# Modulation quarters as TensorE columns, h rounded by ACT from a normalised x, constants on GpSimd's queue, and a halved last block in a macaron transformer layer

## The chip, the core and the metric

The kernel runs on one core of a Trainium2 chip. Its time is the device time of one execution in microseconds (us). The time before is the median of three runs, 2115.29 us (2113.15 to 2115.32). Durations inside the kernel come from the trace of one more execution, which took 2112.17 us.

## The reference

One layer on x of 1024 tokens by 1024 features, all f32. A vector c gives nine modulation vectors of 1024, a shift, a scale and a gate for each of three sub-layers:

```
cond = silu(c)
mod  = (cond @ ada_w + ada_b).reshape(3 sub-layers, 3 kinds, 1024)
h = rms_norm(x, g0) * (1 + scale0) + shift0
x = x + 0.5 * gate0 * swiglu(h)          # 1024 -> 2816 -> 1024
h = rms_norm(x, g1) * (1 + scale1) + shift1
x = x + gate1 * mixer(h)                 # two attentions with 8 heads each
h = rms_norm(x, g2) * (1 + scale2) + shift2
x = x + 0.5 * gate2 * swiglu(h)
```

`rms_norm` divides by the root of the mean square over the features and multiplies by g. Only the modulation of the first sub-layer, its h, and the last addition of the third are touched by the change.

## The kernel before

x is held with features on the partitions: eight blocks c of 128 features, each as two halves of 512 tokens, `x[c][half]`. For precision every operand of a layer matmul is split in two rounded numbers, high and low (`h` for activations, `wh` and `wl` for weights), and a product is three matmuls (`mm3`). The feed-forward layers use a seven-product scheme on quarters of the matrices: `UpPair` computes a pair of blocks of the hidden layer, `Operands` prepares the activations that all pairs share (`b11` is made of blocks 0 to 3 of the first half), `Down` computes the way back in seven passes p of eleven steps q with four output blocks d.

The order of instructions on each engine is made by a planner, `Plan`: while it is on, operations are collected as tasks; `length` prices each of them, `deadlines` and `place` make orders for 34 settings, and the one with the earliest end is issued at `flush`. The first flush holds the whole first feed-forward layer. With `nc.inorder` set, the tasks of SP (its DMA issues) keep the order in which the program names them. Operations named before `nc.on = True` are issued at once in program order. In the profile all planned instructions have line 198, that of `issue`, so groups are told apart by the names of their tiles.

What has to happen before the first matmul of the layer, in `layer`:

- `cond` (c as 128x8) is loaded by SP's queue, `ada_b` and `ng` (the norm's g) by ACT's, and `cond` goes through Silu on ACT.
- SP loads the eight `x[c][0]` (256 KB each), then the pieces of `ada_w`, 256 KB each (`mraw`), and the first halves of the weights `w13a` (`wr`). The pieces of ada_w come in quarters (`ModQuarter`): matrix i (0 is the shift, 1 the scale), columns q*256 to q*256+256, four loads of two 128-row pieces each. Both matrices of quarter q = 0 come first, by turns, then weights of pairs 0 and 1, then q = 1, then weights of pairs 2 and 3.
- `SquareSum` squares x on ACT and adds on VectorE (`nsq`, `nacc`), `norm_rms` sums over the partitions with four matmuls against `ones_col` and takes the inverse root on VectorE (`nv`, `na`, `nr`), `norm_spread` spreads it to all partitions with four matmuls against `ident` into a PSUM bank, `ops.rb[0]`.
- The shift quarter goes through `row`: eight matmuls with a column of `cond` as weight and a piece (256 columns) as moving operand give a row, ACT copies it (`mrow`), two matmuls turn it to columns. The scale quarter goes through `add`: VectorE multiplies each piece by its `cond` and adds up (`macc`, 8 steps), and two matmuls against `ones_col` sum over the partitions. `mod_done` adds `ada_b` and, for a scale, makes A = (mod + 1) * ng.
- `Operands.block` makes `h`: `scale` (VectorE: x = x * A * rb), then ACT rounds x + shift to the high part and VectorE makes the low part.

Blocks 0 and 1 need quarter 0, blocks 2 and 3 quarter 1. Pairs 0 and 1 start in four banks of their own, `y`. Blocks 4 to 7 get their modulation later by `ModHalf`, which is not changed.

At the very end `Down.run` computes pass 6 with the last three steps held back for each block d: for d = 3 these are nine matmuls of 512 columns, then `out` adds the gated result to x on VectorE, and a store of 256 KB to the output follows.

Of the kernel before, what the change touches and what calls it, by code (L numbers as in the profile page):

```python
# [11 lines left out]
F32 = mybir.dt.float32  # L12
F32R = mybir.dt.float32r
# [4 lines left out]
AF = mybir.ActivationFunctionType  # L18
# [39 lines left out]
class View:  # L58


    def __init__(self, tile, ops):
        self.tile, self.ops = tile, ops
# [115 lines left out]
class Plan:  # L178
# [29 lines left out]
    def take(self, engine, op, a, kw, calls=None, took=0.0):  # L208
# [38 lines left out]
        t.left = len(before)  # L247
        out = writes[0] if writes else a[0]
        shape = list(out.shape)
        t.n, t.rows = int(np.prod(shape[1:])), shape[0]  # L250
        if op == "tensor_reduce":
            t.n = int(np.prod(a[1].shape[1:]))
        t.bytes = 4 * int(np.prod(shape))
# [36 lines left out]
    def length(self, t, e):  # L290

        n = t.n
        if t.op == "dma_start":
            return (0.35 if e == "sync" else 0.54), 0.0
        if e == "tensor":
            if t.took:
                return t.took, 0.23
            if t.exact:
                d = max(0.04, 0.003 + n / 2286.0)
            elif t.op == "transpose":  # L300
                d = n / 1174.0
            else:
                d = max(0.224, 0.009 + n / (595.0 if t.rows > 1 else 1200.0))
            return d, 0.23
        more = "accum_out" in t.kw
        if e == "scalar":
            ap = sum(isinstance(t.kw.get(x), View) for x in ("bias", "scale"))
            start = 0.07 if isinstance(t.a[1], View) and t.a[1].tile.pool.space == PSUM else 0.11
            return start + n / 1200.0 + (0.14 if more else 0.0) + (0.06 if ap else 0.0), 0.16
        if e == "gpsimd":  # L310
            if t.op in ("tensor_scalar", "memset"):
                return 0.24 + n / 1190.0, 0.105
            return 0.06 + n / 440.0, 0.105
        if t.op == "tensor_tensor_scan":
            d = 0.15 + n / 480.0
        elif t.op == "tensor_tensor_reduce":
            d = 0.075 + n / 960.0
        elif t.op == "scalar_tensor_tensor" or more:
            d = 0.13 + n / 960.0
        elif t.op == "tensor_scalar" and t.port:  # L320
            d = 0.075 + n / 1920.0
        else:
            d = 0.07 + n / 960.0
        return max(0.2, d), 0.145
# [238 lines left out]
class SquareSum:  # L563
# [5 lines left out]
    def add(self, x):  # L569
        nc = self.k.nc  # L570
        sq = t512(self.k, name="nsq" if self.acc else "nacc")
        nc.scalar.activation(sq, x, AF.Square)
        if self.acc:
            self.eng.tensor_add(self.acc, self.acc, sq)
        else:
            self.acc = sq
        return sq
# [150 lines left out]
def t512(k, dt=F32, name="t", home="c"):  # L728

    p, tag, n = k.homes[home]  # L730
    return p.tile([128, H], dt, tag=tag, name=name, bufs=n)
# [806 lines left out]
class ModQuarter:  # L1538
# [1 line left out]

    N = 256

    def __init__(self, k, i, q, bank):
        self.k, self.i, self.q, self.bank, self.raws = k, i, q, bank, []

    def load(self, g):
        k, n = self.k, self.N
# [3 lines left out]
                            k.ada_w[g * 256:g * 256 + 256, c0:c0 + n].rearrange("(a p) n -> p a n", p=128))  # L1551
        self.raws += [t[:, 0:n], t[:, n:2 * n]]

    def add(self):
        k, nc = self.k, self.k.nc
        acc = t512(k, name="macc")[:, 0:self.N]
        for kc, t in enumerate(self.raws):
            c = k.cond[:, kc:kc + 1]
            if kc == 0:
                nc.vector.tensor_scalar(acc, t, c, None, op0=ALU.mult)  # L1560
            else:
                nc.vector.scalar_tensor_tensor(acc, t, c, acc, op0=ALU.mult, op1=ALU.add)
        self.done(acc, k.ones_col)

    def row(self):
        k, nc = self.k, self.k.nc
        t = self.bank()[0:1, 0:self.N]
        for kc, r in enumerate(self.raws):
            nc.tensor.matmul(t, k.cond[:, kc:kc + 1], r, start=kc == 0, stop=kc == 7)
        r = t512(k, name="mrow")[0:1, 0:self.N]  # L1570
        nc.scalar.activation(r, t, AF.Copy)
        self.done(r, k.ones_col[0:1, :])

    def done(self, v, one):
        t = self.bank()
        for b in range(2):
            self.k.nc.tensor.matmul(t[:, b:b + 1], v[:, b * 128:b * 128 + 128], one, start=True, stop=True)
        mod_done(self.k, self.i, t, 2 * self.q, 2)


def side_by_side(gens):
# [29 lines left out]
class Operands:  # L1611
# [26 lines left out]
    def block(self, c):  # L1638

        self.scale(c, 0)  # L1640
        self.pair("b11" if c < 4 else "b21", self.x[c][0], self.shift(c), "h0")

    def first(self):
        for c0 in (0, 4):
# [235 lines left out]
class Down:  # L1880
# [87 lines left out]
    def run(self, steps={}):  # L1968

        k = self.k  # L1970
        for p, (first, _, early) in enumerate(self.ORDER):
# [8 lines left out]
            new = p in (0, 3)  # L1980
            ops = []

            def mms(d, q):
                w, m = ops[q]
                c = slice(d * 128, d * 128 + 128)
                mm3(k, ps[d], w[0][:, c], w[1][:, c], *m, new and q == 0, q == PAIRS - 1, skip_group_check=True)

            together = PAIRS - self.APART.get(p, 0)
            for q in range(PAIRS):
# [11 lines left out]
                if q < together:  # L2001
                    for d in range(4):
                        mms(d, q)
            for d in range(4):
                for q in range(together, PAIRS):
                    mms(d, q)
                self.out(p, d, ps[d])
                if p == 6 and self.s == 2:
                    self.stores(True)
# [213 lines left out]
def layer(tc, xT, c, pos, ada_w, ada_b, ng, inv, w13a, w2a, w_a, w_f, w_q, w_g, fb, fg, dg, wbr, wout, w13b, w2b, out):  # L2223
    with ExitStack() as es:
# [17 lines left out]
        def const_in(shape, nm, src, eng=nc.sync):  # L2242
            t = cst(shape, F32, nm)
            eng.dma_start(t, src)
            return t

        k.cond = const_in([128, 8], "cond", c)
        k.ada_b = const_in([128, 72], "ada_b", ada_b, nc.scalar)
        k.ng = const_in([128, 24], "ng", ng, nc.scalar)
        nc.scalar.activation(k.cond, k.cond, AF.Silu)  # L2250
        k.ones_col = cst([128, 1], F32, "ones_col")
        nc.vector.memset(k.ones_col, 1.0)
        k.ones_r = cst([128, 1], F32R, "ones_r")
# [35 lines left out]
        with ExitStack() as ph:  # L2289
# [21 lines left out]
                q.first = True  # L2311
            ops = Operands(k, 0, x, nc.vector)
            mod = {i: ModHalf(k, i, 1, bank) for i in range(2)}
            quarter = [[ModQuarter(k, i, q, bank) for i in range(2)] for q in range(2)]
            k.up_step, k.stores = 0, []

            def consts():
# [54 lines left out]
            for i in range(8):  # L2372
                t = sq.add(x[i][0])
                if i < 4:
                    nc.tensor.matmul(warm, z.bitcast(F32)[:, 0:128], x[i][0], start=True, stop=True)
            for n in range(4):
                for m in quarter[0]:
                    m.load(n)
            for i in range(2):
                pairs[i].load1("c", (0,))  # L2380
            for n in range(4):
                for m in quarter[1]:
                    m.load(n)
            for i in range(2, 4):
                pairs[i].load1("c", (0,))
            nc.inorder = False
            rms[0] = norm_rms(k, sq.acc, rp, bank)
            ops.rb[0] = norm_spread(k, rms[0], bank)
            for m in quarter:
                m[1].add()  # L2390
                m[0].row()
            for c in range(4):
                ops.block(c)
            for i in range(4):
                run(i)
            for n in range(8):
# [180 lines left out]
        with ExitStack() as ph:  # L2577
# [57 lines left out]
            for _ in rest:  # L2635
# [3 lines left out]
            next1 = lambda: more(1)  # L2639
            first1 = lambda: [more(1) for _ in range(4)]  # L2640
            down = Down(k, 2, w2b, wq, bank, d_g[1], ["h0"] * 16 + ["h1"] * 16 + ["g"] * 12, lambda t, i, j: nc.sync.dma_start(t, d_x2[i, j]),
                        lambda t, i, j: lambda: nc.sync.dma_start(out[i, :, j * H:j * H + H], t), nc.vector)
            last = side_by_side(ModHalf(k, 8, h, bank).steps(d_row) for h in range(2))
            k.up_step, k.stores = 0, []
            up_all(k, pairs, 3, [(i, n) for i in range(3) for n in range(4)],
# [72 lines left out]
```

## Time and profile before

| | us |
|---|---|
| median of three runs | 2115.29 |
| the profiled execution | 2112.17 |
| its span | 2110.5 |
| TensorE busy | 2094.6 |
| VectorE busy | 1641.7 |
| ACT busy | 1135.6 |
| GpSimd busy | 251.1 |

The page counts busy time of each engine over the span. PE stands for TensorE's matmuls, PEld for its weight loads, DVE for VectorE, POOL for GpSimd, SP for the engine that issues most DMAs. A matmul's end is modelled, so matmuls of 0.39 us that follow one another every 0.23 us overlap in the list. `128x512` is partitions by elements; `out<-in` are tile names. The chain of waits goes back from the last instruction to what released each step.

### The profile page before, as it was taken

Reading aid. Unit: us, or ns where it says so; the run is one execution under the profiler, and the core shown is the slowest. Engines: PE = TensorE matmul, PEld = TensorE weight load, DVE = VectorE, ACT = ScalarE, POOL = GpSimd, SP = SyncE. Lnnn points to the kernel's source line nnn. Section 1 sums busy time; section 2 is a strip of 40 time slices with the busy share of each in tenths; the row PEclk is TensorE's granted clock in tenths of the full one; section 3 lists DMA queues with packets and bytes.
Section 4 is the critical chain, followed back from the end, with each engine's and each line's share of the span. In section 5 each row is a group of like instructions: output and inputs, shape, how many; then the busy total and the mean of one; then the engine's idle time right before and its main releaser. Section 6 shows DMA issues by size and latency. Waiting matters only on the chain.

```text
span 2110.5 us, 30999 instructions
## 1 busy us (share of the span) xinstructions
PE 2094.6 (99%) x10296; PEld 1728.2 (82%) x10296; DVE 1641.7 (78%) x3167; ACT 1135.6 (54%) x2075; POOL 251.1 (12%) x397
## 2 busy tenths in 40 slices
PE   8999999999999999999999999999999999999999
PEld 5887888888888888888888888888888888888887
DVE  7989887869977399886998877979975765568554
ACT  5754444445456266688776776335543333334443
POOL 0022222321100000000444332000000000000000
PEclk9999999999999999999999999999999999999999
DMA  9468888899721555668543224794142523375511
GB/s 347 134 215 275 303 295 274 277 379 366 261 92 48 172 174 192 217 244 274 192 158 99 86 66 160 252 315 154 46 130 100 194 85 129 101 264 206 189 50 41
DMA packets 218285, 398.72 MB, mean 189 GB/s; under 512 B 27198, under 2 KB 69694, under 8 KB 217100
## 3 DMA queue, kind: packets, MB, share of 16 engines
q1 hardware_dynamic: 199772, 339.24, 48.0%
q0 software_dynamic: 18064, 57.46, 7.1%
q8 instruction: 81, 1.33, 0.3%
q14 instruction: 80, 0.66, 0.1%
q10 hardware_dynamic: 288, 0.05, 0.0%
HBM read 282.62 MB, written 114.03 MB: 188 GB/s over the span
## 4 chain that ended last, share of the span: by engine, by line
PE 91%; issue 3%; DVE 2%; DMA 2%; ACT 1%; POOL 1%; SPq 0%; POOLq 0%; DVEq 0%; ACTq 0%
PE b L198 37%; PE y L198 28%; PE pj L198 12%; PE py L198 7%; PE p L198 4%; PE pt L198 4%; DMA mraw<-in_ada_w 0%; POOL d_g L198 0%; DMA f<-d_f 0%; DMA wr<-in_w13b 0%; ACT nt L198 0%; DMA d_wf10l<-pre 0%; DVE z L198 0%; DMA x<-in_xT 0%; ACT h L198 0%
## 5 line engine op out<-in xcount | busy, mean ns | idle before, releaser
L198 PE MATMUL b<-h,wh 128*128 128x512 f32 x1408 | 436.5, 390 | 0.5 <-DVE z L198 0.4
L198 PE MATMUL y<-h,wh 128*128 128x512 f32 x1280 | 397.1, 390 | 0.4 <-ACT h L198 0.3
L198 ACT ACTIVATE wh<-wr 128x512 fp32r<-128x512 f32 x308 | 192.6, 629 | 316.0 <-PE b L198 166.1
L198 PEld LDWEIGHTS b<-h,wh 128*128 128x128 f32 x1408 | 263.2, 188 | 59.1 <-DVE z L198 3.4
L198 PEld LDWEIGHTS y<-h,wh 128*128 128x128 f32 x1280 | 239.6, 188 | 53.4 <-issue 1.2
L198 DVE TENSOR_TENSOR wl<-wr,wh 128x512 fp32r<-128x512 f32 x308 | 208.4, 686 | 94.4 <-ACT wh L198 88.8
L198 PE MATMUL b<-h,wl 128*128 128x512 f32 x704 | 273.6, 389 | 0.0
L198 PE MATMUL y<-h,wl 128*128 128x512 f32 x640 | 249.0, 389 | 0.0
L198 PE MATMUL pj<-wh,h 128*128 128x512 f32 x512 | 161.3, 391 | 0.0
L198 PEld LDWEIGHTS b<-h,wl 128*128 128x128 f32 x704 | 132.2, 188 | 27.7
L198 PEld LDWEIGHTS y<-h,wl 128*128 128x128 f32 x640 | 120.1, 188 | 24.8
L198 ACT ACTIVATE wh<-g 128x512 fp32r<-128x512 f32 x154 | 96.0, 624 | 80.2 <-PE b L198 55.7
L198 PE MATMUL b<-wh 128*128 128x512 f32 x352 | 137.0, 389 | 0.7 <-ACT mrow L198 0.7
L198 DVE TENSOR_TENSOR wl<-a,wh 128x512 fp32r<-128x512 f32 x132 | 90.8, 688 | 59.9 <-ACT wh L198 55.7
L198 PE MATMUL b<-wl,wh 128*128 128x512 f32 x352 | 136.9, 389 | 0.0
L198 PE MATMUL b<-wh,wl 128*128 128x512 f32 x352 | 136.8, 389 | 0.0
L198 ACT ACTIVATE wh<-a 128x512 fp32r<-128x512 f32 x132 | 82.4, 625 | 99.9 <-PE b L198 60.3
L198 DVE TENSOR_TENSOR wl<-g,wh 128x512 fp32r<-128x512 f32 x154 | 105.6, 686 | 29.6 <-ACT wh L198 29.1
L198 POOL TENSOR_SCALAR pr<-pr,mn 128x128 f32<-128x128 f32 (+7 forms) x128 | 102.3, 816 | 167.3 <-DVE mn L198 135.1
L198 ACT ACTIVATE pth<-pt 128x512 fp32r<-128x512 f32 (+1 forms) x160 | 85.5, 554 | 55.9 <-PE pt L198 54.3
L198 DVE TENSOR_TENSOR ptl<-pt,pth 128x512 fp32r<-128x512 f32 (+1 forms) x160 | 97.9, 632 | 20.1 <-ACT pth L198 18.6
L198 PEld LDWEIGHTS pj<-wh,h 128*128 128x128 f32 x512 | 95.7, 188 | 18.6
(382 smaller groups left out, 4376.4 us busy)
## 6 DMA issues: line engine op xcount, KB each, us to landing
g<-d_g SPq DMA_DIRECT2D x154, 256.0 KB, 5.3
mraw<-in_ada_w SPq DMA_DIRECT2D x144, 256.0 KB, 5.7
wr<-in_w13a SPq DMA_DIRECT2D x112, 256.0 KB, 5.4
wr<-in_w13b SPq DMA_DIRECT2D x88, 256.0 KB, 4.8
d_g<-z POOLq DMA_DIRECT2D x77, 256.0 KB, 5.8
d_g<-z SPq DMA_DIRECT2D x77, 256.0 KB, 3.2
a<-in_w2a SPq DMA_DIRECT2D x44, 256.0 KB, 6.3
a<-in_w2b SPq DMA_DIRECT2D x44, 256.0 KB, 5.3
```

What stands on the lines that cost most here:

```text
L198: getattr(getattr(self.tc.nc, engine), op)(*map(real, a), **{n: real(v) for n, v in kw.items()})
```

## The change

```diff
@@ Plan.length, price of a matmul that is not rounded f32
-                d = max(0.224, 0.009 + n / (595.0 if t.rows > 1 else 1200.0))
+                d = max(0.112, 0.005 + n / 1200.0)
@@ class ModQuarter (add, row and done are gone)
+    def columns(self, *banks):
+        k = self.k
+        ts = [bank() for bank in banks]
         for b in range(2):
-            self.k.nc.tensor.matmul(t[:, b:b + 1], v[:, b * 128:b * 128 + 128], one, start=True, stop=True)
-        mod_done(self.k, self.i, t, 2 * self.q, 2)
+            t = ts[b % len(ts)]
+            for kc, r in enumerate(self.raws):
+                k.nc.tensor.matmul(t[:, b:b + 1], r[:, b * 128:b * 128 + 128], k.cond[:, kc:kc + 1], start=kc == 0, stop=kc == 7)
+        for b in range(len(ts)):
+            mod_done(k, self.i, ts[b][:, b:], 2 * self.q + b, 2 // len(ts))
@@ class Operands
+    def normed(self, c):
+        t = self.x[c][0]
+        self.k.nc.vector.tensor_mul(t, t, self.rb[0])
+
+    def rounded(self, c):
+        k, nc, t, i = self.k, self.k.nc, self.x[c][0], self.s * 8 + c
+        scale, shift = k.A[:, i:i + 1], self.shift(c)
+        a, b = t512(k, F32R, "h", "h0"), t512(k, F32R, "h", "h0")
+        nc.scalar.activation(a, t, AF.Identity, bias=shift, scale=scale)
+        self.x[c][0] = x = t512(k, name="x")
+        nc.vector.tensor_scalar(x, t, scale, None, op0=ALU.mult)
+        nc.vector.scalar_tensor_tensor(b, x, shift, a.bitcast(F32), op0=ALU.add, op1=ALU.subtract)
+        k.B["b11"].append((a, b))
@@ Down.run, after the steps that are done together
+                if p == 6 and self.s == 2 and d == 3:
+                    t, g = self.x[d][1], k.G[:, self.s * 8 + d:self.s * 8 + d + 1]
+                    for i in range(2):
+                        cs = slice(i * 256, i * 256 + 256)
+                        for q in range(together, PAIRS):
+                            mms(d, q, (cs,))
+                        k.nc.vector.scalar_tensor_tensor(t[:, cs], ps[d][:, cs], g, t[:, cs], op0=ALU.mult, op1=ALU.add)
+                        self.done(t[:, cs], d, 1, i)()
+                    break
@@ layer
-        k.cond = const_in([128, 8], "cond", c)
-        k.ada_b = const_in([128, 72], "ada_b", ada_b, nc.scalar)
-        k.ng = const_in([128, 24], "ng", ng, nc.scalar)
-        nc.scalar.activation(k.cond, k.cond, AF.Silu)
+        k.cond = const_in([128, 8], "cond", c, nc.gpsimd)
+        k.ada_b = const_in([128, 72], "ada_b", ada_b, nc.gpsimd)
+        k.ng = const_in([128, 24], "ng", ng, nc.gpsimd)
+        k.cond.tile.written = 5.0
...
-            for n in range(4):
-                for m in quarter[0]:
+            for m in quarter[0]:
+                for n in range(4):
                     m.load(n)
...
             nc.inorder = False
+            nc.scalar.activation(k.cond, k.cond, AF.Silu)
             rms[0] = norm_rms(k, sq.acc, rp, bank)
             ops.rb[0] = norm_spread(k, rms[0], bank)
-            for m in quarter:
-                m[1].add()
-                m[0].row()
             for c in range(4):
-                ops.block(c)
+                ops.normed(c)
+            for q in quarter:
+                for m in q:
+                    m.columns(bank, bank)
+            for c in range(4):
+                ops.rounded(c)
```

So each 128-column block of a quarter becomes eight matmuls with the piece as weight and one column of `cond` moving, which sum over all 1024 features in PSUM; each of the two blocks has a bank of its own and its own `mod_done`. x is multiplied by the norm factor before A is known, ACT applies scale and shift while it rounds, and VectorE makes the scaled x in a new tile and the low part from it. The quarters' loads come matrix by matrix (quarter 1 is reordered in the same way). The three constants go through GpSimd's DMA queue, ahead of GpSimd's other work; Silu becomes a planned task that the planner takes to be ready at 5.0 us. In the last block of the kernel the nine held-back matmuls are done for 256 columns, then the addition and the store of that half, then the same for the other half (the store's slice gets an argument for the half). The planner's price for f32 matmuls is halved for all flushes.

More of the change, by code (lines that the diff above doesn't have):

```diff
@@ L249, in take @@
         shape = list(out.shape)
-        t.n, t.rows = int(np.prod(shape[1:])), shape[0]
+        t.n = int(np.prod(shape[1:]))
         if op == "tensor_reduce":
@@ L1541, with __init__ @@
     N = 256
-    def __init__(self, k, i, q, bank):
-        self.k, self.i, self.q, self.bank, self.raws = k, i, q, bank, []
+    def __init__(self, k, i, q):
+        self.k, self.i, self.q, self.raws = k, i, q, []
     def load(self, g):
@@ L1552, in load @@
         self.raws += [t[:, 0:n], t[:, n:2 * n]]
[L1554 to L1575, printed above, removed]
-        for b in range(2):
-            self.k.nc.tensor.matmul(t[:, b:b + 1], v[:, b * 128:b * 128 + 128], one, start=True, stop=True)
-        mod_done(self.k, self.i, t, 2 * self.q, 2)
+    def columns(self, *banks):
+        k = self.k
+        ts = [bank() for bank in banks]
+        for b in range(2):
+            t = ts[b % len(ts)]
[3 more added lines that the diff above has]
+            mod_done(k, self.i, ts[b][:, b:], 2 * self.q + b, 2 // len(ts))
 def side_by_side(gens):
@@ L1981, in run, with mms @@
             ops = []
-            def mms(d, q):
+            def mms(d, q, cut=(slice(0, H),)):
                 w, m = ops[q]
                 c = slice(d * 128, d * 128 + 128)
-                mm3(k, ps[d], w[0][:, c], w[1][:, c], *m, new and q == 0, q == PAIRS - 1, skip_group_check=True)
+                for s in cut:
+                    mm3(k, ps[d][:, s], w[0][:, c], w[1][:, c], m[0][:, s], m[1][:, s], new and q == 0, q == PAIRS - 1, skip_group_check=True)
             together = PAIRS - self.APART.get(p, 0)
@@ L2313, in layer @@
             mod = {i: ModHalf(k, i, 1, bank) for i in range(2)}
-            quarter = [[ModQuarter(k, i, q, bank) for i in range(2)] for q in range(2)]
+            quarter = [[ModQuarter(k, i, q) for i in range(2)] for q in range(2)]
             k.up_step, k.stores = 0, []
@@ L2380, in layer @@
                 pairs[i].load1("c", (0,))
-            for n in range(4):
-                for m in quarter[1]:
+            for m in quarter[1]:
+                for n in range(4):
                     m.load(n)
@@ L2641, in layer @@
             down = Down(k, 2, w2b, wq, bank, d_g[1], ["h0"] * 16 + ["h1"] * 16 + ["g"] * 12, lambda t, i, j: nc.sync.dma_start(t, d_x2[i, j]),
-                        lambda t, i, j: lambda: nc.sync.dma_start(out[i, :, j * H:j * H + H], t), nc.vector)
+                        lambda t, i, j, h=None: lambda: nc.sync.dma_start(out[i, :, j * H:j * H + H] if h is None else out[i, :, j * H + h * 256:j * H + h * 256 + 256], t), nc.vector)
             last = side_by_side(ModHalf(k, 8, h, bank).steps(d_row) for h in range(2))
```

## The prediction

> **What bounds the kernel now.** I read the page first, then the table by stage, then the chain of waits of the first 65 us and TensorE's part of the timeline there, and last the end.
>
> ```profile
> span 2110.5 us, 30999 instructions
> PE 2094.6 (99%) x10296; PEld 1728.2 (82%) x10296; DVE 1641.7 (78%) x3167; ACT 1135.6 (54%) x2075; POOL 251.1 (12%) x397
> ```
>
> The span is TensorE's: 99% busy, so only two things can move the time, TensorE's own work and the few places where it idles. The table by stage (stretch, its length, then busy time and count for PE, PEld, DVE, ACT, POOL) says where those are:
>
> ```profile
> 0.00:20.00 20.00, 14.70 (x54) 7.37 (x55) 12.63 (x37) 9.37 (x15) 1.16 (x7) 1.00 0.91 300
> 400.00:660.00 260.00, 259.30 (x1150) 213.20 (x1149) 210.90 (x354) 144.54 (x257) 41.67 (x75) 1.00 0.70 247
> 1200.00:1300.00 100.00, 98.45 (x754) 83.45 (x751) 77.09 (x179) 75.79 (x165) 34.95 (x46) 1.00 0.22 65
> ```
>
> TensorE idles 5.3 us of the first 20; later the worst stretch of the feed-forward has 0.7, the worst of the attention 1.55. What the change edits lies in the first 38 us and in the last 5. The chain of waits at the start (start, length, what):
>
> ```profile
> 9.32 6.03 DMA mraw<-in_ada_w
> ...
> 18.95 0.17 DVE mod L198
> ...
> 19.34 0.76 DVE x L198
> 20.12 0.73 ACT h L198
> 20.89 0.73 PE y L198 x2
> ...
> 37.95 23.41 PE b L198 x115
> ```
>
> The first matmul of the layer proper starts at 20.89, behind the last load of the first quarter of `ada_w`, the sums over it, `mod`, `A`, the scaling of x and its rounding. From 20.89 to 37.95 TensorE does these layer matmuls, with the second quarter's sums between them:
>
> ```profile
> L198 PE MATMUL y<-h,wh 128*128 128x512 f32 x32 | 11.2, 407 | 0.3 <-ACT h L198 0.3
> L198 PE MATMUL y<-h,wl 128*128 128x512 f32 x16 | 6.4, 398 | 0.0
> L198 PE MATMUL b<-h,wh 128*128 128x512 f32 x4 | 1.2, 390 | 0.0
> L198 PE MATMUL b<-h,wl 128*128 128x512 f32 x2 | 0.8, 391 | 0.0
> L198 PE MATMUL b<-mraw,cond 128*1 128x256 f32 x12 | 3.1, 378 | 0.0
> L198 PE MATMUL b<-ones_col,mrow 1*128 1x1 f32 x4 | 0.6, 250 | 0.0
> L198 PE MATMUL b<-ones_col,macc 128*128 128x1 f32 x4 | 0.5, 229 | 0.0
> ```
>
> One such matmul costs, in a dense stretch (chain of waits, late):
>
> ```profile
> 1986.86 59.84 PE b L198 x264
> ```
>
> 59.84 / 264 = 0.227 us. The 54 of the first four rows above are 12.24 us of the 17.06 up to 37.95; of the other 4.82, the second quarter (last three rows) took 4.2 and gaps 0.6. So I keep one account, TensorE's debt: how long it was not doing layer matmuls before it became dense. Before: 37.95 - 12.24 = 25.7 us. After 37.95 the change touches nothing until the end, so the head's effect on the time is the new debt minus 25.7.
>
> **The change part by part.** *Quarters as columns.* The shift quarter was a row: eight matmuls with a one-column weight and 256 moving columns. The scale quarter was summed on VectorE. Now each block of 128 columns of each piece is the weight and one column of `cond` moves: 2 blocks x 8 pieces x 4 quarters = 64 matmuls on TensorE. The timeline has both forms:
>
> ```profile
> 10.95 1.02 PE L198 MATMUL b<-mraw,cond 128*1 128x256 f32 x4 [1.16 <-DMA mraw<-in_ada_w]
> 12.05 1.05 PE L198 MATMUL b<-ones_col,nacc 128*128 128x1 f32 x8
> 17.41 1.16 PE L198 MATMUL b<-ident,nr 128*128 128x128 f32 x8
> 47.53 1.84 PE L198 MATMUL b<-ones_col,macc 128*128 128x1 f32 x16
> 49.23 0.72 PE L198 MATMUL b<-h,wh 128*128 128x512 f32 x2
> ```
>
> The rows at 47.53 are 8 instructions in the code and 16 records: an f32 matmul counts twice. They take 49.23 - 47.53 = 1.70 us, 0.2125 us for one; the new columns have just this form (128x128 f32 weight, one column). 64 x 0.2125 = 13.6 us, 6.8 for each pair of quarters. The Trainium skill, "TensorE: Matmul & The Clock Gate", section "Back-to-back issue gap", puts a stream of weight loads and matmuls at about 81 ns each for 128 moving columns. By that the 128 records would take an estimated 10.4 us, 3.2 less, and the forecast would fall by as much; this trace has 106 ns for a record with an f32 weight, and decides.
>
> What goes: 16 row matmuls (four records of them took 1.02 us at 10.95, so 8 us in all, over half of it before 20.89) and the small matmuls behind rows and sums. VectorE's 16 steps of the sums go too, 14 of them 0.48 us (row below): worth nothing by themselves, because TensorE is dense from 20.89 on.
>
> New debt: the first column can start when the first piece has landed. Loads are issued in order by SP:
>
> ```profile
> 0.81 0.39 SPq L198 DMA_DIRECT2D cond<-in_c  x1
> 1.25 3.75 SPq L198 DMA_DIRECT2D x<-in_xT  x8
> ```
>
> With `cond` off this queue all of it moves up by 1.25 - 0.81 = 0.44 us: first piece at 10.95 - 0.44 = 10.5. The seventh landed at 15.35 (chain), 0.73 us apart, so the eighth at 16.1, now 15.7. TensorE has to do by then: 32 columns 6.8, the sum of squares 0.98 (12.05 to 13.03), the spread of the norm factor about 1.0 (1.16 with its modelled end): 8.8 us, ending at 19.3 without a pause. That is 3.6 us past the last landing: the first quarter now waits for TensorE's weight loads, where it waited for DMA and VectorE.
>
> Behind this comes the second quarter, 6.8 us, in place of the 4.2; the gaps of 0.6 I carry over, with 0.3 more because eight pieces now come between layer matmuls where five groups did. Between the last column and the first operand (next part) 0.8 us pass, which the second quarter's first piece can fill if it has landed; I take half, 0.4, as idle. Sum: 10.5 + 8.8 + 6.8 + 0.9 + 0.4 = 27.4, or 1.7 us more than 25.7. Bounds: with no idle and no more gaps than before 26.7 (+1.0); with 0.8 idle and twice the gaps, 28.7 (+3.0).
>
> *Norm factor ahead, h rounded by ACT.*
>
> ```profile
> L198 ACT ACTIVATE nt<-nt,mod,A 128x512 f32<-128x512 f32 x16 | 12.8, 808 | 6.1 <-DVE nt L198 6.1
> L198 ACT ACTIVATE h<-x,mod 128x512 fp32r<-128x512 f32 x12 | 8.5, 719 | 3.3 <-DVE x L198 2.8 <-DVE h L198 0.4
> L198 DVE SCALAR_TENSOR_TENSOR macc<-mraw,cond,macc x16: 477/484/752, 12.3 to 34.9; 128x256 f32<-128x256 f32 x14, 128x512 f32<-128x512 f32 x2
> ```
>
> Between `mod` (18.95) and the first layer matmul (20.89) were 1.94 us. The VectorE step of 0.78 leaves this chain (x times the norm factor no longer needs `A`), ACT pays 0.09 for its second pointer (808 - 719): 1.25 remain. The first block's column ends at least two matmuls (0.43) before the last one, hence the 0.8 of gap above. It also needs weights: by the spacing the first piece of `w13a` lands 0.73 behind the quarter, at 16.4, in time to be rounded. VectorE gets one more operation for each of four blocks (scaling by `A`; at most the 0.75 of the widest row above, 3 us in all), beside TensorE's columns, while it has lost 14 x 0.48 = 6.7 us of sums: nothing on the path.
>
> *Constants on GpSimd's queue; Silu after the squares.* Three small loads wait behind nothing there, but push GpSimd's `zr` and `ident` back by three issues (0.39 us for one on SP, above; none is shown on GpSimd this early, and I allow it 1 us), to 4 us at most; the seeds of the banks need `zr`, and TensorE has nothing that presses before 10.5.
>
> ```profile
> d_g<-z POOLq DMA_DIRECT2D x77, 256.0 KB, 5.8
> ```
>
> A whole 256 KB through that queue takes 5.8 us; `cond` would be there by 6.6 at the worst, 3.9 us before the first column. Added wait: Silu now sits between ACT's squares; squares queue behind it if `cond` is late, and so do VectorE's sum of them and the norm factor. From the sum of squares (12.05) to the spread (17.41) were 5.4 us; with the columns ending at 19.3 the spread has about 1.9 us to spare. So 0; at worst, `cond` at 6.6 and a reload of ACT's function table for Silu, +1.
>
> *Last block in two halves.*
>
> ```profile
> 2106.15 0.39 PE L198 MATMUL y<-wh,wl 128*128 128x512 f32 x1
> 2106.57 0.75 DVE L198 SCALAR_TENSOR_TENSOR xc<-y,G,xc 128x512 f32<-128x512 f32 x1 [1.29 <-PE y L198]
> out_dram<-xc SPq DMA_DIRECT2D x4, 256.0 KB, 2.0
> ```
>
> The end is the last matmul, one addition over 512 columns, one 256 KB store. In halves the final addition covers 256: 0.75 - (0.75 - 0.48) by the `macc` row's two forms, 0.27 less. The store of 128 KB saves half of its transfer; loads of this size land 0.73 us apart, so about 0.35. TensorE pays 18 matmuls of 256 for 9 of 512: the same stream, unless a weight load (0.106) no longer hides under 0.113, so 0 to +0.1. Sum -0.6 (bounds -0.65, and -0.2 if the landing time is all latency).
>
> *The planner's price* for an f32 matmul falls from 0.224 to 0.112 us, while the trace has 0.2125. It therefore plans the columns at half their length, and it re-plans all it flushes. Outside the head TensorE idles little (0.7 and 1.55 us in the worst stretches above), so a new order can win little; I allow -2 to +3, centre 0.
>
> **The sum.** +1.7 - 0.6 = +1.1 us. The profiled execution took 2112.17 us for its span of 2110.5; it would become 2113.3. The median of the runs shown, 2115.29, is 3.1 above it, and the forecast goes on the median: 2116.4 us, 0.05% up. What a measurement of this kernel can tell from no change is about 0.2%, 4.2 us: faster is below 2111.1, slower above 2119.5.
>
> **Rivals.**
>
> *The columns hide behind the loads* (faster side). If TensorE gave one column for 0.106 us, or the record pairs overlapped, the first quarter would end with its last landing (15.7), layer matmuls begin near 17.2, and the second quarter cost 3.4: debt 17.2 + 3.4 + 0.9 = 21.5, -4.2; with the end's -0.6 it is 2110.5. For it: TensorE's idle 5.3 us in the head. Against: 16 records in 1.70 us, with nothing else in between.
>
> *The clock falls during the columns* (slower). Early in this trace TensorE ran at half rate, whatever the clock column says:
>
> ```profile
> 5.53 0.34 PEld L198 LDWEIGHTS b<-x,zr 128*128 128x128 f32 x1 [0.52 <-DMA x<-in_xT]
> 6.38 0.34 PEld L198 LDWEIGHTS b<-x,zr 128*128 128x128 f32 x1 [0.52 <-issue]
> 7.91 0.19 PEld L198 LDWEIGHTS b<-x,zr 128*128 128x128 f32 x1 [0.34 <-issue]
> 8.34 0.19 PEld L198 LDWEIGHTS b<-x,zr 128*128 128x128 f32 x1 [0.24 <-issue]
> ```
>
> The same loads came 0.85 us apart at first and 0.43 later, 0.34 and 0.19 us long. If eight us of one-column matmuls do not count as work, the rate can halve again among them. Halfway, at 14.9, the 4.4 us left until 19.3 would double, and layer matmuls run at half rate for at least the 1.9 us that the slow rows above span (5.53 until a switch near 7.4), +1.0: +5.4, 2121.8. It passes 2119.5 once the fall comes before 17. Against: the 8 such records at 12.05 and 16 at 47.53 slowed nothing behind them, but they were short. The Trainium skill, same page, Part 1, says that the clock follows how busy the array was in windows of about 3.4 us; it does not say how a one-column matmul counts, and no run here shows it.
>
> *The new order misses elsewhere*: the half-priced columns make plan and chip drift 6.8 us apart, and a bank or buffer comes late in the first feed-forward. A drift in which VectorE or a store holds TensorE for three such stretches as that from 1200 costs 3 x 1.55 = 4.6 us, 2121.0; a lucky order could give back as much in the attention, 2111.8.
>
> **How the numbers follow.** Forecast with its bounds 0.68; columns hidden 0.08; clock 0.10; order 0.14, split evenly. The forecast's own range, from its bounds (+1.0 - 0.65 - 2 and +3.0 - 0.2 + 1 and part of the order's +3), is -1.7 to +4.5: 2113.6 to 2119.8. To leave out no more than 2 in 10 it reaches to the other cases: 2111 to 2121. Faster: hidden 0.06 (the rest of it stays above 2111.1), lucky orders that save in the feed-forward as well 0.05, the forecast's edge 0.01: 0.12. Slower: clock 0.08, order 0.05, the forecast's edge 0.03: 0.16. The rest, 0.72, is no difference.
>
> **What would show it.** Right: 128 records `b<-cond,mraw` or the like at 0.106 us, dense from about 10.5 to 19.3; first layer matmul near 20.1; rows `mrow` and 256-wide `macc` gone; debt near 27.4; at the end an addition of 0.48 us and a landing of 1.7. Wrong: a first layer matmul before 18 or TensorE waiting for DMA between columns (hidden); weight loads of 0.3 us between 14 and 25 (clock); idle of over 2 us between 40 and 1300 that was not there (order).

## The result and the profile after

The changed kernel takes 2139.2 us (median of four, 2135.33 to 2142.33), the kernel before beside it 2114.22: a ratio of 1.0118, 95% interval 1.0098 to 1.0138, so 25 us slower. The forecast was 2116.4, 1.1 over the time before, with a range to 2121. The profiled execution is the slowest of the four: 2142.33 us, span 2140.6, 30.1 more than before.

The table by stage of the changed kernel (stretch, length, busy time and count of PE, PEld, DVE, ACT, POOL, then TensorE's granted clock, DMA share, GB/s):

```profile
0.00:20.00 20.00, 15.79 (x71) 12.26 (x72) 7.62 (x25) 8.21 (x12) 2.97 (x10) 0.89 0.93 305
20.00:32.00 12.00, 10.68 (x45) 9.79 (x44) 6.93 (x15) 3.60 (x6) 0.00 (x0) 0.50 1.07 375
32.00:40.00 8.00, 8.00 (x35) 7.52 (x33) 0.93 (x3) 0.00 (x0) 0.00 (x0) 0.50 1.05 387
40.00:60.00 20.00, 20.00 (x79) 17.01 (x79) 13.00 (x25) 8.19 (x14) 0.00 (x0) 0.76 0.65 215
60.00:80.00 20.00, 20.00 (x101) 16.95 (x100) 16.43 (x36) 14.26 (x26) 0.00 (x0) 1.00 0.67 195
```

Before, the row of the second stretch was:

```profile
20.00:32.00 12.00, 11.73 (x51) 6.77 (x50) 9.71 (x22) 3.97 (x7) 0.00 (x0) 1.00 1.08 374
```

The third column from the end is the news: 0.50 where before it was 1.00. A mean of 0.89 over the first 20 us puts the fall near 15.5, one of 0.76 from 40 to 60 the return at 49.6 (the trace's own clock records say 15.48 and 49.61). For 34 us TensorE ran at half rate while its busy column says that it was fully at work. The same on TensorE's timeline (start, length, what):

```profile
11.20 1.02 PE L198 MATMUL b<-cond,mraw 128*128 128x1 f32 x8 [0.49 <-DMA mraw<-in_ada_w]
12.09 1.05 PE L198 MATMUL b<-ones_col,nacc 128*128 128x1 f32 x8
13.00 6.01 PE L198 MATMUL b<-cond,mraw 128*128 128x1 f32 x38
18.87 2.06 PE L198 MATMUL b<-ident,nr 128*128 128x128 f32 x8
20.72 3.84 PE L198 MATMUL b<-cond,mraw 128*128 128x1 f32 x18
25.73 2.16 PE L198 MATMUL y<-h,wh 128*128 128x512 f32 x3 [1.18 <-ACT h L198]
27.69 1.70 PE L198 MATMUL b<-cond,mraw 128*128 128x1 f32 x8
29.25 0.77 PE L198 MATMUL y<-h,wl 128*128 128x512 f32 x1
```

Eight column records take 1.02 us at 11.20 and 1.70 at 27.69; a layer matmul is 0.77 long at 29.25, where 0.39 is its length at full rate. From the first layer matmul at 25.73 until the clock returns TensorE does this (groups, 25.7 to 49.75):

```profile
L198 PE MATMUL b<-cond,mraw 128*128 128x1 f32 x64 | 13.6, 332 | 0.0
L198 PE MATMUL y<-h,wh 128*128 128x512 f32 x17 | 10.0, 682 | 1.3 <-ACT h L198 1.2
L198 PE MATMUL y<-h,wl 128*128 128x512 f32 x6 | 4.4, 726 | 0.0
```

The debt is 49.8 - 23 x 0.227 = 44.6 us against 25.7: +18.9. Of this, 34.1 us at half rate are up to 17.1 us lost, and 1.8 remain for the added work, where the forecast had 1.7.

The other 11.2 us come later. Two marks, the first products with `wa` (end of the first feed-forward) and with `yh` (first of the mixer's output part); before, then after (name, count, shortest, median, longest ns, first and last start us):

```profile
L198 PE MATMUL b<-wa,h x192: 352/360/466, 637.2 to 707.5; 128*128 128x432 f32 x192
L198 PE MATMUL b<-yh,wh x64: 389/389/391, 1308.1 to 1389.1; 128*128 128x512 f32 x64
```

```profile
L198 PE MATMUL b<-wa,h x192: 352/360/469, 663.1 to 733.7; 128*128 128x432 f32 x192
L198 PE MATMUL b<-yh,wh x64: 388/389/396, 1336.7 to 1417.7; 128*128 128x512 f32 x64
```

The distance is 25.9 at the first mark, 28.6 at the second, 30.1 at the end: 7.0 us lost between 50 and 663, 2.7 in the projections and attention, 1.5 after. Of the 2.7, up to 1.7 are a second, short fall of the clock, which the trace before does not have:

```profile
1329.60:1333.10 3.50, 3.50 (x11) 2.74 (x10) 1.58 (x3) 1.32 (x3) 0.60 (x1) 0.51 0.84 239
```

The end of the changed kernel (timeline):

```profile
2133.89 0.28 PE L198 MATMUL y<-wh 128*128 128x256 f32 x1
...
2135.20 0.28 PE L198 MATMUL y<-wh,wl 128*128 128x256 f32 x1
2135.51 0.48 DVE L198 SCALAR_TENSOR_TENSOR xc<-y,G,xc 128x256 f32<-128x256 f32 x1 [0.68 <-PE y L198]
2136.05 0.39 PE L198 MATMUL y<-wh 128*128 128x256 f32 x1 [0.58 <-DVE xc L198]
...
2136.75 0.28 PE L198 MATMUL y<-wh,wl 128*128 128x256 f32 x1
2137.07 0.48 DVE L198 SCALAR_TENSOR_TENSOR xc<-y,G,xc 128x256 f32<-128x256 f32 x1 [1.07 <-PE y L198]
```

Twelve 256-column matmuls go by, 0.119 us apart (the code has nine for each half, so three of these belong to the second), and then TensorE waits until the addition has read the first half of the bank: 0.85 us from 2135.20 to 2136.05, where 0.12 was due. Why the last six, which write the other half, have to wait for it is not shown.

### The profile page after: what moved, and what is told of

Same layout as the page of the kernel before. It is cut to its first block, busy times and chain, and to the rows that moved or that the text cites. A ratio compares the mean times of both kernels' runs of the same rounds, so it can differ in the third digit from the quotient of the medians.

```text
span 2140.6 us, 31210 instructions
## 1 busy us (share of the span) xinstructions
PE 2116.9 (99%) x10385; PEld 1755.2 (82%) x10385; DVE 1633.6 (76%) x3162; ACT 1135.2 (53%) x2074; POOL 251.9 (12%) x400
## 4 chain that ended last, share of the span: by engine, by line
PE 86%; issue 7%; DMA 2%; DVE 2%; POOL 2%; ACT 1%; SPq 0%; POOLq 0%; DVEq 0%; ACTq 0%
PE b L198 34%; PE y L198 25%; PE pj L198 12%; PE py L198 7%; PE p L198 4%; PE pt L198 4%; POOL d_g L198 1%; DMA wr<-in_w13b 0%; DVE z L198 0%; DMA nat<-d_qkv 0%; ACT nt L198 0%; DMA d_wg2l<-pre 0%; DMA d_wf10l<-pre 0%; DMA mraw<-in_ada_w 0%; DMA d_wf23l<-pre 0%
```

## The experiments

Three theories. C: one-column matmuls do not keep TensorE's clock up. O: the halved price makes an order in which plan and chip drift apart. P: one of the other parts is what costs. For all kernels the debt (time less 0.2267 us, 59.84 / 264, for each layer matmul up to then) at 60 us, which is the head's, and at 660, which adds the first feed-forward, worked out from the grouped rows of each profile:

| kernel | debt at 60 | at 660 | time, us | ratio to before, 95% |
|---|---|---|---|---|
| before | 28.5 | 39.7 | 2112.6 to 2114.2 | |
| changed | 44.6 | 64.5 | 2139.2 | 1.0118 (1.0098 to 1.0138) |
| rows_back | 29.6 | 45.0 | 2118.03 | 1.0032 (1.0019 to 1.0045) |
| columns_only | 46.6 | 61.5 | 2134.09 | 1.0105 (1.0090 to 1.0120) |
| price_back | 45.9 | 57.7 | 2132.09 | 1.0093 (1.0076 to 1.0110) |
| price_only | 37.1 | 49.3 | 2123.66 | 1.0048 (1.0035 to 1.0061) |
| ahead_only | 34.8 | 45.9 | 2119.01 | 1.0026 (1.0016 to 1.0037) |
| ahead_gpsimd | 29.2 | 40.4 | 2114.46 | 1.0006 (0.9997 to 1.0015) |
| tail_only | | | 2114.03 | 1.0002 (0.9993 to 1.0012) |
| warm_fill | 38.5 | 72.4 | two groups, below | |
| fill_price | 59.1 | 86.9 | two groups, below | |

**rows_back.** The changed kernel with the old quarters.

```diff
-            for q in quarter:
-                for m in q:
-                    m.columns(bank, bank)
+            for m in quarter:
+                m[1].add()
+                m[0].row()
... (ModQuarter gets add, row and done back)
```

> The changed kernel with only the quarters' arithmetic as before (shift quarter as a row, scale quarter summed on VectorE); order of loads, constants, rounding, halved last block and the planner's halved price stay as changed. Theory C (one-column matmuls do not keep TensorE's clock up; it halves until they are over): clock 1.00 after 10 us everywhere, debt of the head back to 24 to 27, 2113 to 2118 us. Theory O (the halved price makes an order that chip and plan disagree on): still 2130 or more, as the price is still halved. Theory P (one of the other parts is what costs): still 2130 or more.

2118.03, 5.4 over the kernel before beside it: 19.6 of the 25 us are gone. Against the expectation the clock is not 1.00 throughout: it dips once, where it does not in the trace before (stretch 18 to 22 and the next):

```profile
18.00:22.00 4.00, 3.37 (x15) 2.49 (x16) 2.64 (x10) 1.23 (x3) 0.00 (x0) 0.64 1.11 349
22.00:26.00 4.00, 4.00 (x14) 1.17 (x12) 3.96 (x9) 1.26 (x2) 0.00 (x0) 0.93 1.08 372
```

TensorE had idled before it, from 14 to 18 it was busy for 2.3 us, and 256-column rows brought the clock back within 4 us. The columns are the cause of most; O and P as whole explanations fall. Of the 5 us left (debt +5.3 at 660, only +1.1 of it at 60) most belong to the halved price: ahead_gpsimd below, which is this kernel with the old price and the whole last block, is at 1.0006.

**columns_only.** The kernel before with the columns alone.

```diff
-            for m in quarter:
-                m[1].add()
-                m[0].row()
+            for q in quarter:
+                for m in q:
+                    m.columns(bank, bank)
... (ModQuarter gets columns in place of add, row and done)
```

> The kernel before with only the quarters' arithmetic as columns, everything else as before, the planner's price too. Theory C: granted clock 0.5 from about 17 us until the second quarter is done (40 to 50 us), debt +15 to +20, 2130 to 2140 us. Theory O: with the true price the order fits; debt +1 to +2, 2115 to 2118 us. Theory P: 2115 to 2118 us.

2134.09, with a debt of +18.1 at 60, as C has it, but the clock does not fall among the columns. TensorE waits here for the norm factor before the first column:

```profile
11.78 1.05 PE L198 MATMUL b<-ones_col,nacc 128*128 128x1 f32 x8 [1.61 <-DVE nacc L198]
15.36 2.05 PE L198 MATMUL b<-ident,nr 128*128 128x128 f32 x8 [2.53 <-DVE nr L198]
17.20 7.04 PE L198 MATMUL b<-cond,mraw 128*128 128x1 f32 x33
```

The clock falls in that gap, at 15.2, and all the columns run at half rate until it returns near 49.4. An idle stretch takes it down, and the columns do not bring it back. In the changed kernel, where columns fill TensorE from 13.00 on, they take it down themselves.

**price_back.** The changed kernel with the old price.

```diff
-                d = max(0.112, 0.005 + n / 1200.0)
+                d = max(0.224, 0.009 + n / (595.0 if out_rows(t) > 1 else 1200.0))
```

> The changed kernel with only the planner's price for f32 matmuls as before (0.224 us). Theory C: the columns still come in a row, the clock still halves: 2130 to 2142 us. Theory O: 2115 to 2118 us.

2132.09: the head is no better (45.9), the rest is: from 60 to 660 the debt grows by 11.8 as in the kernel before (11.2), with the halved price by 19.9. So the 7 to 8 us between the head and the end of the feed-forward belong to the price; in time it is 5.5 us, +19.5 here against +25.0 for the changed kernel, each over the kernel before beside it.

**price_only.** The kernel before with the halved price.

```diff
-                d = max(0.224, 0.009 + n / (595.0 if t.rows > 1 else 1200.0))
+                d = max(0.112, 0.005 + n / 1200.0)
```

> The kernel before with only the planner's price for f32 matmuls halved; the operations are the same, only their order differs. From the traces so far (debt at 660 us: 45.0 with rows and the halved price against 39.7 before; 64.5 against 57.7 with columns): +3 to +7 us, 2115 to 2120, by waits later than 60 us. If the price matters only together with columns or the other parts: 0 to +1.

2123.66, 10 us slower, and not by late waits: the debt is 8.6 higher at 60 already. The new order puts every row behind the spread of the norm factor:

```profile
12.06 1.45 PE L198 MATMUL b<-ones_col,nacc 128*128 128x1 f32 x8 [1.53 <-DVE nacc L198]
17.42 2.05 PE L198 MATMUL b<-ident,nr 128*128 128x128 f32 x8 [3.91 <-DVE nr L198]
...
28.17 1.20 PE L198 MATMUL y<-h,wh 128*128 128x512 f32 x4 [1.91 <-ACT h L198]
```

TensorE idles for 3.9 us before 17.42, the clock is at 0.81 in the mean of the first 20 us and 0.84 in the next (together 14 us at half rate), and the first layer matmul comes at 28.17 instead of 20.89. The expectation was too low, 2120 at most, and had the place wrong.

**warm_fill.** The changed kernel with columns of zeros moved behind each column matmul.

```diff
+                k.nc.together(0.4, ("matmul", (t[:, b:b + 1], r[...], k.cond[:, kc:kc + 1]), ...),
+                              ("matmul", (t[:, 128:512], k.zr[:, 0:128], k.zr[:, 128:512]), dict(start=False, stop=False, ...)))
...
-            z = t512(k, F32R, "zr")
+            k.zr = z = t512(k, F32R, "zr")
```

> The changed kernel with one more matmul of 384 moving columns of zeros (rounded f32, its result in unused columns of the same bank, never read) behind each of the 64 columns: 64 x 0.16 = 10.2 us more work for TensorE in the head at full rate. Theory C: the clock stays at 1.00, the debt at 60 us is about 38 instead of 44.6, and the kernel is faster than the changed one by 4 to 10 us although it does more, 2126 to 2135. Theory O and P: the added work is paid in full, 10 us slower than the changed kernel, 2146 to 2152.

The profiled execution keeps its clock through all columns (10 to 38 us at 1.00, two of the stretches):

```profile
14.00:18.00 4.00, 4.00 (x34) 4.00 (x33) 2.48 (x10) 1.30 (x3) 0.00 (x0) 1.00 1.07 374
34.00:38.00 4.00, 4.00 (x31) 4.00 (x31) 3.57 (x8) 0.82 (x1) 0.00 (x0) 1.00 1.05 386
```

Its debt at 60 is 38.5, six less than the changed kernel's with 10 us more work: C's number. The time missed: 2149.95 and 2153.17 in two executions (mean clock 0.996 and 0.995), 2173.18 and 2176.65 in two others (0.984). From 400 to 660 the debt grows by 24 in the profiled one, above all from 440 to 560, where DMA moves 354 to 376 GB/s without a break. There TensorE idles for 12.8 us behind ACT (7.8 for weights rounded late, 5.0 for a row), and behind these waits the clock falls three times, for 17 us in all:

```profile
520.00:560.00 40.00, 32.17 (x124) 24.86 (x123) 36.39 (x60) 17.00 (x31) 9.02 (x16) 0.87 1.02 376
```

This is another order, and not the columns. The two groups, some 23 us apart in one and the same kernel, fit a clock kept or lost in the head: 0.0115 of 2160 us, over 0.5, is 50 us of half rate, 25 us lost. The slower two have no trace.

**fill_price.** The same with the old price, by the lines of price_back.

> The filled kernel (384 columns of zeros moved behind each column of the quarters) with the old price: the order trouble of the filled kernel between 400 and 560 us should go with the price, so that the time shows the clock alone. Theory C: clock 1.00 in the head, debt at 60 us 37 to 39 against 45.9 with the old price and no filler, 2124 to 2128, that is 4 to 8 us faster than that kernel's 2132 with 10 us more work. Theory O and P: 2140 or more.

2154.44 once (mean clock 0.993), 2168.91 to 2173.68 three times (0.984 to 0.986). Here the profiled execution lost the clock, at 15.7:

```profile
20.00:60.00 40.00, 40.00 (x158) 39.70 (x159) 16.77 (x37) 4.29 (x6) 0.00 (x0) 0.50 0.79 275
```

and did not regain it in 43 us of the same stream that warm_fill ran through at full rate in 27. The expectation failed: the filler is not enough to hold the clock always, and the price did not remove the waits either (10.4 us of idle from 480 to 600). In this stream, at full rate, 0.17 of 0.40 us, 43%, move columns.

**block_columns and block_rows.** The kernel before with a block of one form in the dense last feed-forward, where nothing waits.

```diff
+            t, g = bank(), k.ident
+            nc.together(13.6, *[("matmul", (t[:, 0:1], g, k.ones_col), dict(start=True, stop=True)) for _ in range(64)])
```

```diff
+            t, g = bank(), down.g[0, 0]
+            nc.together(14.7, *[("matmul", (t[0:1, 0:256], k.ones_col, g[:, 0:256]), dict(start=True, stop=True)) for _ in range(32)])
```

> The kernel before with a block of 64 one-column f32 matmuls (128x128 weight, one moving column, results not used) put as one piece among the dense matmuls of the last feed-forward: nothing in the head changes, and no load or other engine waits on it. At full rate it is 13.6 us of TensorE. Theory C: a few us into the block the granted clock falls to 0.5, the records go from 0.106 to 0.21 us apart, and the layer matmuls behind the block run at half rate for some us before the clock returns: +20 to +27 us. Theory O and P: clock 1.00, +13.6.

> The same with 32 f32 matmuls of a one-column weight and 256 moving columns (the form of the old shift row), 14.7 us of TensorE at 0.46 us each. All theories: clock 1.00 throughout, +14 to +15 us; if the clock falls here too, it is not the short moving side that counts.

+25.0 us for the columns, +13.9 for the rows (2138.67 and 2127.52 against 2113.65), as C has it. The columns' block on TensorE's timeline, and by stretches:

```profile
1898.57 22.84 PE L198 MATMUL b<-ones_col,ident 128*128 128x1 f32 x128
1921.27 0.77 PE L198 MATMUL b<-wh 128*128 128x512 f32 x1
```

```profile
1900.00:1902.00 2.00, 2.00 (x20) 2.00 (x19) 1.97 (x4) 0.00 (x0) 0.00 (x0) 1.00 1.06 398
1902.00:1904.00 2.00, 2.00 (x18) 2.00 (x17) 1.14 (x2) 0.00 (x0) 0.00 (x0) 0.87 1.04 397
1904.00:1906.00 2.00, 2.00 (x11) 2.00 (x11) 0.00 (x0) 0.00 (x0) 0.00 (x0) 0.50 0.98 349
1926.00:1928.00 2.00, 2.00 (x7) 1.53 (x7) 0.94 (x2) 1.15 (x2) 0.00 (x0) 0.66 0.00 0
```

The fall comes at 1903.5, 4.9 us into the block; it takes 22.7 us instead of 13.6, and the layer matmuls behind it run at half rate for 6 more. The rows' stretch:

```profile
1900.00:1914.00 14.00, 14.00 (x66) 5.33 (x65) 4.48 (x8) 0.63 (x1) 0.00 (x0) 1.00 1.03 380
```

Same engine, same operand type, as long: full clock in the block. (In the head of this trace, which the edit does not touch, the clock falls once, for the 3.4 us from 20.4 on; the trace before does not have that.) This settles C without head, order or waits. It does not yet tell few moving columns from full weights.

**bursts.** The same 64 column matmuls in four bursts of 16.

```diff
+            def burst():
+                t, g = bank(), k.ident
+                nc.together(3.4, *[("matmul", (t[:, 0:1], g, k.ones_col), dict(start=True, stop=True)) for _ in range(16)])
...
-                    18: [next1]}, lambda: down.loads(down.LEAD), ...)
+                    18: [next1], 40: [burst], 60: [burst], 80: [burst], 100: [burst]}, lambda: down.loads(down.LEAD), ...)
```

> The kernel before with the same 64 one-column f32 matmuls as in block_columns (results not used), but in four bursts of 16 (3.4 us each) some 100 us apart among the dense matmuls of the last feed-forward's first part. In block_columns the clock fell 4.9 us into the block. If the length of an unbroken run of one-column matmuls decides: clock 1.00, +13 to +16 us. If any of them takes the clock down for some us: as much as the one block, +20 or more.

```profile
1547.47 4.72 PE L198 MATMUL b<-ones_col,ident 128*128 128x1 f32 x32
1646.80 3.63 PE L198 MATMUL b<-ones_col,ident 128*128 128x1 f32 x32
1705.08 3.63 PE L198 MATMUL b<-ones_col,ident 128*128 128x1 f32 x32
1764.21 3.63 PE L198 MATMUL b<-ones_col,ident 128*128 128x1 f32 x32
```

2131.81 against 2112.61, +19.2: between the two answers. The first burst loses the clock on its way, at 1549.78, for 6.8 us. The other three run through at full rate, but behind the fourth the layer matmuls run at half rate for 3.4 us:

```profile
1764.00:1768.24 4.24, 4.24 (x36) 4.12 (x35) 3.67 (x6) 1.12 (x2) 0.00 (x0) 1.00 0.45 158
1768.24:1771.65 3.41, 3.41 (x9) 2.64 (x8) 0.00 (x0) 0.00 (x0) 0.00 (x0) 0.50 0.87 249
```

With 13.6 us of work and half of 10.2 us lost that makes 18.7 of the 19.2. So two bursts of four cost the clock, and 3.4 us without a break can be enough, and need not be. The Trainium skill, "TensorE: Matmul & The Clock Gate", Part 1, has the clock decided over windows of 3.4 us that run freely beside the kernel. This trace agrees as far as the lengths go, 6.8 and 3.4 us of half rate.

**block_mix.** Each of the 64 followed by 512 columns of zeros.

```diff
+            nc.together(28.2, *[c for _ in range(64) for c in (("matmul", (t[:, 0:1], g, k.ones_col), ...),
+                                                               ("matmul", (t2, z[:, 0:128], z), ...))])
```

> The kernel before with the 64 one-column matmuls of block_columns in one block, each followed by a rounded f32 matmul of 512 columns of zeros (results not used): 64 x (0.2125 + 0.227) = 28.1 us at full rate, of which 52% move columns. In warm_fill 43% kept the clock in two executions and lost it in two. If the share of time in which columns move decides, with a threshold near 40%: clock 1.00, +28 us. If one-column matmuls take the clock down whatever stands between: +45 us or more.

```profile
1905.00:1915.00 10.00, 10.00 (x67) 9.04 (x68) 0.00 (x0) 0.00 (x0) 0.00 (x0) 1.00 1.01 367
```

2142.63, +30.0, clock 1.00 throughout the block's 29 us. A pair takes 0.46 us in the trace, not 0.44, so columns move for 49% of the time. The weight loads are those of block_columns, so it is the want of moving columns that takes the clock down.

**ahead_only.** The kernel before with `normed` and `rounded` in place of `block`, nothing else.

```diff
+            for c in range(4):
+                ops.normed(c)
             for m in quarter:
                 m[1].add()
                 m[0].row()
             for c in range(4):
-                ops.block(c)
+                ops.rounded(c)
```

> The kernel before with only the norm factor ahead of A and h rounded by ACT; rows, constants, price and end as before. Prediction: the chain from mod to the first layer matmul loses 0.69 us (0.78 of VectorE less 0.09 for ACT's second pointer), so the first one at 20.2 instead of 20.9: -0.7 us at most, 2112 to 2114; a new order may take it back. Theory P for this part: over +3.

2119.01: a miss, 5.7 us slower. The chain got shorter, the order worse: rows stand behind the spread again, TensorE waits 3.6 us for the norm factor, and the clock goes with it.

```profile
14.00:18.00 4.00, 1.13 (x5) 1.16 (x6) 3.82 (x16) 0.92 (x2) 0.00 (x0) 0.50 1.08 373
```

**ahead_gpsimd.** Norm ahead, rounding, constants on GpSimd's queue, Silu planned, loads matrix by matrix; rows, old price, whole last block. Against ahead_only:

```diff
+        k.cond = const_in([128, 8], "cond", c, nc.gpsimd)
...
-            for n in range(4):
-                for m in quarter[0]:
+            for m in quarter[0]:
+                for n in range(4):
                     m.load(n)
...
+            nc.scalar.activation(k.cond, k.cond, AF.Silu)
```

> The kernel before with the norm factor ahead, rounding by ACT, the constants on GpSimd's queue, Silu planned and the loads matrix by matrix; rows and sums, the old price and the whole last block. Theory C: clock 1.00 from 10 us on, debt at 60 us 27 to 29, 2111 to 2115 us: the rest of the change is worth about nothing either way. Theory P: over 2118.

2114.46, no difference; the debt of 29.2 is just over the range. Against the expectation the clock is not 1.00 from 10 us on: it falls once, for 3.4 us:

```profile
18.00:22.00 4.00, 3.85 (x18) 2.03 (x18) 3.93 (x11) 2.82 (x5) 0.00 (x0) 0.63 1.10 348
```

The parts that aren't columns, price or the last block are worth nothing either way in this order; in that of ahead_only two of them cost 5.7 us. No version tried beats the kernel before.

**tail_only.** The kernel before with the halved last block.

```diff
+                if p == 6 and self.s == 2 and d == 3:
...
+                        self.done(t[:, cs], d, 1, i)()
+                    break
```

> The kernel before with only the last block in two halves. By the changed kernel's trace (second half waits for the addition on the first; 256-wide matmuls 0.119 us apart instead of 0.113; landing 0.1 shorter, addition 0.27 shorter): +0.3 to +0.6 us. By the prediction: -0.6.

1.0002: within the interval, -1.5 to +2.5 us, it can be any of the two sizes. The traces decide. From the first of the held-back matmuls of the last block to the end are 6.71 us in the changed kernel (2133.89 to 2140.6) and 6.61 in tail_only (2105.71 to 2112.32), before 6.17 (2106.15 less eight steps of 0.227, to 2110.5).

**What the traces add up to.** The 15 traces hold more than the stretches shown. In each of them all changes of the clock, from first to last, lie whole multiples of 3.413 us apart: the half rate in the head lasts 34.13 us, ten times that, in the changed kernel, columns_only and price_back alike. So every trace can be cut into such windows, and for each window the share of time in which columns move can be counted from the matmuls' records (at full rate 0.443 ns for a column of a rounded matmul, 0.227 / 512, and 0.84 for one of a plain f32 record, by the prediction's row at 10.95, (1.02 - 0.38) / 3 for 256 columns; at half rate twice that). Of the windows at full rate from 8 to 2100 us, the 28 behind which the clock fell have shares of 0.00 to 0.39, the 9072 behind which it stayed 0.40 to 1.00. At half rate, the 51 behind which it stayed low have at most 0.67, but for one of 0.75, the 28 behind which it rose at least 0.71. It matters little why a share is low: 0.00 in columns_only is waiting, 0.01 in the changed kernel (12.07 to 15.48) are columns.

That accounts for what bursts and fill_price left odd. The bursts' starts fall differently into the windows: 0.33 and 0.14 for the two that cost the clock, at least 0.43 for the others. And a stream of 43% holds a clock that is up and does not raise one that is down. fill_price lost it in the window from 12.28 to 15.69, with a share of 0.37, in which the last one-column matmuls of the sum of squares stand before the filled columns; in warm_fill the windows lie otherwise, and the lowest in its stream has 0.41. This count was made on the traces at hand, with some records missing from them, and no run was made to test it.

## Why the prediction was wrong, point by point

*The step that failed* is the price of the columns: the sum takes all 64 at 0.2125 us (6.8 + 6.8) and the layer matmuls among them at 0.227, that is at full rate. They ran at half rate, from 15.5 to 49.6, which cost 17 us where the sum has none. The mechanism was named as a rival, "the clock falls during the columns", but with a chance of 0.10 and a price of +5.4. The price was too small because I let the half rate end with "at least the 1.9 us" of layer matmuls behind the first quarter. But the second quarter's columns stand between the layer matmuls: in the windows from 18.9 to 46.2 columns move for at most 0.50 of the time, and the clock came back only behind 3.4 us of layer matmuls alone. The chance was too small because the evidence against it was weak: the eight and sixteen records that "slowed nothing behind them" last 1.0 and 1.7 us, half a window at most, as the prediction itself half said ("but they were short"), and the block needed 4.9.

*The columns' own cost* comes out at 1.8 us of debt besides the clock, forecast 1.7. It is a remainder: the 17 us take all of the 34 for work, while TensorE idled for 1.3 of them, and the terms behind it did not come as forecast (next point). That it agrees to a tenth is in part luck. The 0.2125 itself holds: at full rate 16 of them take 3.63 us with the last one's modelled end.

*The start* came otherwise: the first column came at 11.20 and waited 0.49 us for its load, forecast 10.5; and the first layer matmul at 25.73, forecast 20.1, by the halved rate and because the spread was placed behind 46 column records.

*The halved price*: allowed for with -2 to +3 and "a new order can win little". By itself it costs 10 us (price_only), 8.6 of it in the head, and with the columns 5.5 (price_back), later. The second step that failed is that idle time in the present order bounds what another order costs. It bounds only what one can win.

*Norm factor ahead*: from `A` at 24.68 to the first layer matmul at 25.73 are 1.05 us, from `A` at 19.14 to 20.89 before 1.75: 0.70 shorter, forecast 0.69. In time that is worth nothing that shows: ahead_gpsimd, which has it, is at 1.0006.

*The constants* cost nothing, as forecast, for the reason given. The bound was nearly used: Silu now comes behind the first squares, and a second load of ACT's table stands before it (the trace before has one, at 1.73).

```profile
5.19 1.28 ACT L198 ACT_TABLE_LOAD   x1
...
6.49 0.21 ACT L198 ACTIVATE cond<-cond 128x8 f32<-128x8 f32 x1
```

The sum of squares still started at 12.09 (12.05 before).

*The last block*: the addition shrank from 0.75 to 0.48 as forecast. The matmuls of 256 came 0.119 us apart, 0.1 us in all, the bound; what was not in the sum is the new wait on the addition, 0.7 us, and the store of a half lands after 1.8 us in the changed kernel, 0.2 sooner where 0.35 was forecast. The forecast of -0.6 was +0.5 in the changed kernel's trace and +0.4 in tail_only's.

Open: where exactly between the shares counted the clock turns, and whether the rule holds for other kinds of matmul; no run was made to test it. Why the filled kernels starve between 440 and 600 us was read off the stages and waits only, not tried.

## What to carry to other kernels

Weigh work that goes to TensorE by how long it moves columns, not by whether the engine is busy: one-column matmuls with full weights look 100% busy, and a run of 3.4 us of them can halve the clock (it did twice in four) for itself and for all that is woven into it. Read the granted clock of every stretch before trusting durations from another stretch. And where a planner makes the order, price a change of its cost model as an edit of its own: what it can lose is not bounded by the idle time that the present order shows.

## What the runs showed of the hardware

The clock records of the 15 traces know two values, 1.00 and 0.50, and change at whole multiples of 3.413 us; the means of a stretch lie between. A block of one-column f32 matmuls at full density took the clock down after 4.9 us; bursts of 3.4 us did so twice in four. Rows of 256 moving columns held it for 14 us and raised it within about 4 us; a mix in which columns move for 49% of the time held it for 29 us; one with 43% held it for 27 us in one execution and stayed at half rate for 43 us in another. Counted by windows, it fell behind shares of moving columns up to 0.39 and stayed behind shares from 0.40 on; it rose behind shares from 0.71 on, though not behind one of 0.75. After the columns, dense layer matmuls needed 6.1 us in the block (1921.3 to 1927.4) until full rate was granted. A gap of 2.5 us in which TensorE waited, with a short run of column sums before it, was enough to lose it (columns_only).
